# First norm of a two-block forward pass: order of the squares' adds, engine of one weight split, place of the norm's spread

## The chip, the cores and the metric

The kernel runs on one core of one Trainium2 chip. The metric is the device time of one execution in microseconds (us), as a median of several runs. The core has a matrix engine (TensorE, PE in the profile), a vector engine (VectorE, DVE), an activation engine (ScalarE, ACT), a general engine (GpSimd, POOL) and a queue that starts transfers (SyncE, SP). Each engine works through its own list of instructions in order, and semaphores hold an instruction back until what it needs is there.

## The reference

A sequence of 512 tokens of width 1024 goes through two blocks. Only the beginning of the first block is touched by the change:

```python
h = rmsnorm(x, ln1[l])
z = jnp.einsum('btd,de->bte', h, w_in[l])
u_pool, gq, gk, gv, gg, ga, fq, fk, fv, ff = jnp.split(z, pts, axis=-1)
y_pool = pool_mixer(u_pool, w_pool[l], pool_scale[l])
y_gla = gla_mixer(gq, gk, gv, gg, ga, w_a_up[l], b_a[l], gla_gn[l])
y_fox = fox_mixer(fq, fk, fv, ff, b_f[l])
mix = jnp.concatenate([y_pool, y_gla, y_fox], axis=-1)
x = x + jnp.einsum('btd,de->bte', mix, w_o[l])
```

`rmsnorm` divides each token by the root of the mean of its squares and multiplies by a gain. `gq`, `gk`, `gv` are the query, key and value of a gated linear attention, `ga` is the low-rank input of its decay gate, which is multiplied by `w_a_up`. The rest (a feed-forward layer, a second block with two more attentions) is left as it is.

## The kernel before, in words

Activations lie transposed: 8 tiles of 128 channels by 512 tokens, `x0` to `x7`. Every fp32 operand of a product is split in two: a rounded high part, made by ScalarE (L188), and the remainder, made by VectorE or GpSimd (L189), so that one product costs three matmuls (high by high, low by high, high by low). A weight slab (128 by 1024) is loaded by SyncE into one of two raw buffers `wr`, then split into `wh` and `wl`, of which there are three each (`weight`, L194 to L203). By default every second slab has its remainder made on GpSimd, the others on VectorE (`share` is 2 there). A raw buffer is free for the next transfer when both halves of its split are done.

The norm is not applied before the products. The products run on x times the gain, and their results are multiplied by the reciprocal root afterwards. For that the squares are summed: ScalarE squares each tile (L294, L297), VectorE adds seven of them into `ss` (L298), TensorE sums `ss` over its channels with eight one-column matmuls against `ones` (`col_sum`), ScalarE and VectorE make the reciprocal root `col` and split it in two `part` tiles (`inv_sqrt`, `parts`), TensorE spreads it over the 128 partitions with eight matmuls against `identr` (`spread`), and ScalarE copies the result to a tile `R` (L280). `R` multiplies every product by channel, `col` every product by token.

TensorE's order is written out by hand. Products on the first slabs run while the sums are made: the small slab of the gates (`psg`), the query slab (`psq`), then five of the eight steps of the key slab (`XS`); then the column sums; then the rest of the key slab, with the spread in between; then the value product by token (`gla_v`), whose slab is in two halves `w1gv`. After the first two steps of it (six matmuls) comes the matmul of the gate, `ga` by `wau`, which needs `R`: VectorE adds the two halves of the gate product into a tile `b` (L581), and multiplies it by `R` into `ga` (L582).

The other engines' lists are ordered by a scheduler, which works with modelled times, with two means to move it: `high_priority`, and `issue_after`, which queues an instruction behind a given one on its engine.

Of the kernel before, what the change touches and what calls it, by code (L numbers as in the profile page):

```python
# [11 lines left out]
F32 = mybir.dt.float32  # L12
# [4 lines left out]
OP = mybir.AluOpType  # L17
# [67 lines left out]
class Body:  # L85
# [179 lines left out]
    def parts(self, c):  # L265

        n = c.shape[1]
        hi, lo = (self.gp.tile([P, 8], F32R, tag="part", name="part", bufs=6)[:, :n] for _ in "hl")
        self.nc.vector.tensor_copy(hi, c)
        self.nc.vector.tensor_tensor(lo, c, hi.bitcast(F32), op=OP.subtract)  # L270
        return hi, lo

    def spread(self, parts):

        ps = self.bank("tr")
        for t in range(NT):
            for a, c in enumerate(parts):
                self.mm(ps[:, t * P:(t + 1) * P], c[:, t:t + 1].to_broadcast([P, P]), self.identr, a == 0, a == 1)
        r = self.row()
        self.nc.scalar.activation(r, ps, AF.Copy)  # L280
        return r

    def rstd(self, sums, n):
        with self.tc.high_priority():
            c = self.inv_sqrt(self.col_sum(sums)[0], n)
            parts = self.parts(c)
        yield RSW
        with self.tc.high_priority():
            return self.spread(parts), c

    def square_into(self, ssum, src, first, scale=1.0, eng=None):
        nc = self.nc
        if first:
            nc.scalar.activation(ssum, src, AF.Square, scale=scale)  # L294
        else:
            sq = self.tmp()
            nc.scalar.activation(sq, src, AF.Square, scale=scale)  # L297
            (eng or nc.gpsimd).tensor_tensor(ssum, ssum, sq, op=OP.add)  # L298

    def acts(self):  # L300
        return [tuple(self.hp.tile([P, T], F32R, name=f"{c}{k}", tag=f"{c}{k}") for c in ("hh", "hl"))
# [172 lines left out]
    def block1(self, ctx, raw):  # L474
        nc, A, x = self.nc, self.A, self.x
        mp = self.pool(ctx, "mix")
        mix = [tuple(mp.tile([P, T], F32R, name=f"m{c}{k}") for c in "hl") for k in range(4)]
        b = lambda dt=F32: mp.tile([P, T], dt, tag="b", name="b", bufs=NB)

        wg = self.wp.tile([P, 1024], F32R, tag="wh", name="wh", bufs=3)  # L480
        wg3, raw3 = wg.rearrange("p (k m) -> p k m", m=P), raw[:, :512].rearrange("p (k m) -> p k m", m=64)
        self.split(wg3[:, :, :64], wg3[:, :, 64:], raw3)
        rq = self.wp.tile([P, 1024], F32, tag="wr", name="wr", bufs=WR)
        wq = [self.wp.tile([P, 1024], F32R, tag=t, name=t, bufs=3) for t in ("wh", "wl")]
        h = self.acts()
        ssum = self.sums()
        for k in range(KD):
            for n, at in enumerate((XA, XB)):
                if k == at:
                    cols = slice(n * 512, n * 512 + 512)  # L490
                    nc.sync.dma_start(rq[:, cols], A["w1s"][T1["gq"]][:, cols])
                    self.split(*(w[:, cols] for w in (*wq, rq)))
            nc.sync.dma_start(x[k], A["xT"][k * P:(k + 1) * P, :])
            last = nc.scalar.activation(h[k][0], x[k], AF.Identity, scale=self.gain("ln1", k))
            nc.vector.scalar_tensor_tensor(h[k][1], x[k], self.gain("ln1", k), h[k][0].bitcast(F32),  # L495
                                           op0=OP.mult, op1=OP.subtract)
        self.ident = self.const(self.gp, "ident", [P, P])
        self.identr = self.gp.tile([P, P], F32R, name="identr")
        nc.scalar.activation(self.identr, self.ident, AF.Copy)
        for k in range(KD):  # L500
            with self.tc.issue_after(getattr(last, "ins", last)):
                self.square_into(ssum, x[k], k == 0, eng=nc.vector)
        self.identb = self.const(mp, "identb", [P, P], BF16)
        self.causalb = self.const(mp, "causalb", [P, P], BF16)
        psg = self.bank("mm")
        gen = self.dense(wq, h)
        for k in range(KD):
            for half in (True, False) if k == KD - 1 else (False, True):
                if half:
                    self.mm(psg[:64], wg3[:, k, :64], h[k][1], False, False)  # L510
                else:
                    self.mm(psg, wg3[:, k, :], h[k][0], k == 0, k == KD - 1)
            if k >= XL:
                next(gen)
        psq = self.all(gen)
        gen = self.dense(self.slab("w1s", T1["gk"]), h)
        for _ in range(XS):
            next(gen)
        r = self.rstd([ssum], D)
        next(r)  # L520
        next(gen)
        next(gen)
        R, Rc = self.all(r)
        psk = self.all(gen)
        fd = self.dp.tile([8, T], F32, name="fd")
        V = [[], []]
        proj = self.fox_proj(h, R, b)
        with ExitStack() as c:
            self.gla_phase(c, h, R, Rc, mix, mp, b, fd, psg, (psq, psk), V, proj)
        self.share = 1  # L530
        with ExitStack() as c:
            xp = self.pool(c, "mix2")
            mix += [tuple(xp.tile([P, T], F32R, name=f"m{c}{k}") for c in "hl") for k in range(4, KD)]
            self.fox_phase(mp, b, mix, V, fd, proj, self.half_zero(xp))
            self.share = 2
            h2 = self.acts()
            ssum = self.sums()
            for m in range(KD):
                self.all(self.w_o(mix, m, 1))
                self.split_scaled(h2[m][0], h2[m][1], x[m], self.gain("ln2", m))  # L540
                self.square_into(ssum, x[m], m == 0, eng=nc.vector if m == KD - 1 else nc.gpsimd)
            self.last = [ssum]
        self.h = h2
# [8 lines left out]
    def gla_phase(self, ctx, h, R, Rc, mix, mp, b, fd, psg, held, V, proj):  # L552
        nc, A = self.nc, self.A
# [23 lines left out]
        def gates():  # L577

            z, t = new()[:64], self.tmp()[:64]
            nc.scalar.activation(t, psg[64:], AF.Copy)  # L580
            nc.vector.tensor_tensor(z, psg[:64], t, op=OP.add)  # L581
            nc.vector.tensor_tensor(ga, z[:16], R[:16], op=OP.mult)  # L582
            f = new()[:8]
            nc.vector.tensor_tensor(f, z[32:40], R[32:40], op=OP.mult)
            F = self.log_sigmoid(f, self.gain("b_f", 0, 8), 8, new)
            one = new()[:8]
            nc.gpsimd.memset(one, 1.0)
            nc.vector.tensor_tensor_scan(F, one, F, 0.0, op0=OP.mult, op1=OP.add)
            nc.sync.dma_start(fd, F)

        def gla_v():
            yield from self.take()
            w = [self.weight(A["w1gv"][a]) for a in range(2)]
            for t in range(NT):
                ps = yield from self.token_major(h, t, w)
                nc.vector.tensor_scalar(gv[t], ps[:, :256], Rc[:, t:t + 1], None, op0=OP.mult)
                if t < NT - 1:
                    yield
            self.busy = False
# [117 lines left out]
        def chain(f, held=None):  # L717
            if f == 0:
                gates()
            q, k = yield from qk(f, held)  # L720
            yield QKW
            r = decay(f, q, k)
            yield DECW
            sb = yield from state(f, r)
            gs[f] = yield from gate(f)
            yield GOW
            yield from output(f, r, sb, gs[f])
# [28 lines left out]

        self.spawn(chain(0, held))
        self.later("gv", gla_v(), 2 * UNIT)
        self.spawn(chain(1), CH1)
        self.spawn(pooling(0), PL0)  # L760
# [718 lines left out]
```

## Time and profile before

| | us |
|---|---|
| three runs | 1077.87, 1076.41, 1077.69 |
| median | 1077.69 |
| the profiled execution, its own time | 1081.27 |
| its span, first to last instruction | 1079.5 |
| TensorE busy in it | 1048.9 (97%) |
| VectorE busy in it | 671.8 (62%) |
| ScalarE busy in it | 545.5 (51%) |
| GpSimd busy in it | 366.8 (34%) |

Mean granted TensorE clock is 0.990 of full speed. A row of the timeline gives the start from the span's beginning, the duration, the engine, the line, the operation with the tiles written and read, and in brackets the idle time before it with what ended it. Rows of several instructions (x3) are merged: their duration runs from the first start to the last end. Matmuls overlap each other, so the distance between starts tells their pace, not their duration.

### The profile page before, as it was taken

To read this page: it belongs to the slowest core of one execution; us is meant where nothing else is said; L and a number is where in the kernel's file an instruction comes from. 1 tells how busy PE (TensorE), PEld (TensorE's weight loads), DVE (VectorE), ACT (ScalarE), POOL (GpSimd) and SP (SyncE) were. 2 spreads that over 40 slices of the span, in tenths; PEclk is the share of its full clock that TensorE was granted. 3 is DMA by queue.
4 is the path that set the end of the run, shared out by engine and by line. 5 is a ranking of instruction groups with operands and counts; after the bars stand their busy time and mean duration, and the time that the engine had idled before them with its cause. 6 is when DMAs were issued, how large, how long until landed. Compare 5 with 4: busy or idle time off the path is not lost.

```text
span 1079.5 us, 14066 instructions
## 1 busy us (share of the span) xinstructions
PE 1048.9 (97%) x5264; PEld 868.8 (80%) x5264; DVE 671.8 (62%) x1140; ACT 545.5 (51%) x954; POOL 366.8 (34%) x214
## 2 busy tenths in 40 slices
PE   8999999999999999999999998989899999999997
PEld 6888877788888888888888787768787898888786
DVE  6653488885545423454533278999995566888652
ACT  6763578755323211333244465656565556778233
POOL 1233322143222100232223243443334336655354
PEclk9999999999999999999999999989999999999999
DMA  6312132152222232323223143232232323335842
GB/s 229 99 59 79 63 102 64 66 185 98 98 98 97 83 104 84 110 89 102 88 95 108 40 144 131 90 108 88 74 100 86 117 78 118 109 99 163 287 144 79
DMA packets 41692, 114.84 MB, mean 106 GB/s; under 512 B 4952, under 2 KB 9448, under 8 KB 41624
## 3 DMA queue, kind: packets, MB, share of 16 engines
q1 hardware_dynamic: 38536, 107.62, 30.6%
q10 hardware_dynamic: 2448, 4.22, 1.0%
q0 software_dynamic: 640, 2.10, 0.5%
q8 instruction: 42, 0.69, 0.3%
q14 instruction: 26, 0.21, 0.1%
HBM read 103.40 MB, written 13.14 MB: 108 GB/s over the span
## 4 chain that ended last, share of the span: by engine, by line
PE 79%; DVE 14%; ACT 2%; issue 2%; DMA 1%; SPq 0%; DVEq 0%; ACTq 0%
PE mm L151 67%; PE sc L151 4%; PE pv L151 3%; PE tr L151 2%; PE tr L158 2%; DVE kst L189 2%; DVE score L1016 1%; DVE m L1015 1%; DVE pl L387 1%; DVE b L311 1%; DVE b L374 1%; DVE qk L189 1%; DVE s L369 1%; DVE s L1069 1%; DVE b L369 1%
## 5 line engine op out<-in xcount | busy, mean ns | idle before, releaser
L189 POOL TENSOR_TENSOR wl<-wr,wh 128x1024 fp32r<-128x1024 f32 (+2 forms) x107 | 262.5, 2454 | 565.7 <-ACT wh L188 525.6
L151 PE MATMUL mm<-hh,wh 128*128 128x512 f32 (+2 forms) x808 | 325.5, 403 | 1.6 <-DVE z L1087 1.6
L151 PE MATMUL mm<-hl,wh 128*128 128x512 f32 (+3 forms) x808 | 316.9, 392 | 0.5 <-DVE hl L495 0.5
L151 PE MATMUL mm<-hh,wl 128*128 128x512 f32 (+1 forms) x800 | 314.3, 393 | 0.0
L188 ACT ACTIVATE wh<-wr 128x1024 fp32r<-128x1024 f32 (+2 forms) x142 | 146.8, 1034 | 217.1 <-PE mm L151 181.8
L151 PEld LDWEIGHTS mm<-hh,wh 128*128 128x128 f32 (+1 forms) x808 | 153.4, 190 | 33.4 <-DVE z L1087 2.0
L151 PEld LDWEIGHTS mm<-hh,wl 128*128 128x128 f32 (+1 forms) x800 | 151.2, 189 | 32.8
L151 PEld LDWEIGHTS mm<-hl,wh 128*128 128x128 f32 (+2 forms) x808 | 152.9, 189 | 28.7 <-DVE hl L495 1.2
L151 PE MATMUL mm<-fh,wdh 128*128 128x512 f32 x176 | 70.1, 398 | 0.0
L151 PE MATMUL mm<-fl,wdh 128*128 128x512 f32 x176 | 69.6, 395 | 0.0
L151 PE MATMUL mm<-fh,wdl 128*128 128x512 f32 x176 | 69.6, 395 | 0.0
L188 ACT ACTIVATE wdh<-wd 128x1408 fp32r<-128x1408 f32 x16 | 22.1, 1381 | 72.1 <-PE mm L151 68.1
L875 DVE TENSOR_TENSOR u<-mm,R 128x512 f32<-128x512 f32 x22 | 15.2, 691 | 68.3 <-PE mm L151 68.3
L880 DVE TENSOR_TENSOR x<-mm,x 128x512 f32<-128x512 f32 x16 | 11.1, 692 | 73.3 <-PE mm L151 73.3
L387 DVE TENSOR_TENSOR pl<-tr,ph 128x128 fp32r<-128x128 f32 (+1 forms) x96 | 46.0, 483 | 11.3 <-ACT ph L386 10.2
L189 DVE TENSOR_TENSOR fl<-u,fh 128x512 fp32r<-128x512 f32 x22 | 42.1, 1914 | 14.7 <-ACT fh L188 14.7
L371 ACT ACTIVATE s<-s,m 128x128 f32<-128x128 f32 (+1 forms) x64 | 35.7, 558 | 25.5 <-DVE m L369 25.2
L298 POOL TENSOR_TENSOR ss<-ss,t 128x512 f32<-128x512 f32 x21 | 30.8, 1479 | 52.0 <-ACT t L297 51.9
L189 DVE TENSOR_TENSOR wl<-wr,wh 128x1024 fp32r<-128x1024 f32 (+1 forms) x34 | 40.8, 1199 | 9.4 <-ACT wh L188 9.3
L151 PE MATMUL mm<-wh,hh 128*128 128x256 f32 x160 | 46.5, 290 | 0.0
L151 PE MATMUL mm<-wl,hh 128*128 128x256 f32 x160 | 45.2, 283 | 0.0
L386 ACT ACTIVATE ph<-tr 128x128 fp32r<-128x128 f32 (+1 forms) x96 | 40.5, 427 | 9.4 <-PE tr L158 8.7
(341 smaller groups left out, 2019.1 us busy)
## 6 DMA issues: line engine op xcount, KB each, us to landing
wr<-in_w1gu SPq DMA_DIRECT2D x44, 512.0 KB, 3.5
wr<-in_w2s SPq DMA_DIRECT2D x39, 512.0 KB, 3.5
wd<-in_w1d SPq DMA_DIRECT2D x16, 704.0 KB, 4.2
wr<-in_w1s SPq DMA_DIRECT2D x15, 512.0 KB, 3.5
wr<-in_w1o SPq DMA_DIRECT2D x8, 512.0 KB, 3.5
wr<-in_w2o SPq DMA_DIRECT2D x8, 512.0 KB, 3.8
shear<-gd SPq DMA_DIRECT2D x1, 2560.0 KB
x<-in_xT SPq DMA_DIRECT2D x8, 256.0 KB, 4.9
```

The costliest lines, as they stand in the source:

```text
L151: self.nc.tensor.matmul(out, l, r, start=start, stop=stop)
L158: self.nc.tensor.transpose(out, src, self.ident if ident is None else ident)
L188: self.nc.scalar.activation(hi, src, AF.Copy)
L189: (eng or self.nc.vector).tensor_tensor(lo, src, hi.bitcast(F32), op=OP.subtract)
L298: (eng or nc.gpsimd).tensor_tensor(ssum, ssum, sq, op=OP.add)
L311: nc.vector.tensor_tensor(q[x:x + 64], qf[o:o + 64], q[o:o + 64].bitcast(F32), op=OP.subtract)
L369: nc.vector.tensor_tensor_reduce(out=s[:, :n], in0=sc[:, :n], in1=bias(i), op0=OP.add, op1=OP.min, scale=1.0, scalar=3e38, accum_out=m[:, ...
L371: nc.scalar.activation(s[:, :n], s[:, :n], AF.Exp, scale=-1.0, bias=m[:, 0:1], accum_out=m[:, 1:2])
L386: nc.scalar.activation(hi, trv, AF.Copy)
L387: nc.vector.tensor_tensor(lo, trv, hi.bitcast(F32), op=OP.subtract)
L875: nc.vector.tensor_tensor(u, ps, self.R2, op=OP.mult)
L880: nc.vector.tensor_tensor(x[m], ps, x[m], op=OP.add)
```

## The change

Three edits, all in the first 30 us. The adds of the squares get high priority. The two halves of the value slab are both split on VectorE (`pool=False`), the first behind the last add of a square, the second behind the split of the reciprocal root; the gate's add `b` is put behind that split too. And the spread of the root is issued after the third part of the products (the whole key slab) instead of before its last step.

```diff
     def parts(self, c):
...
-        self.nc.vector.tensor_tensor(lo, c, hi.bitcast(F32), op=OP.subtract)
+        last = self.nc.vector.tensor_tensor(lo, c, hi.bitcast(F32), op=OP.subtract)
+        self.parted = getattr(last, "ins", last)
         return hi, lo
...
     def square_into(self, ssum, src, first, scale=1.0, eng=None):
...
-            (eng or nc.gpsimd).tensor_tensor(ssum, ssum, sq, op=OP.add)
+            return (eng or nc.gpsimd).tensor_tensor(ssum, ssum, sq, op=OP.add)
...
         for k in range(KD):
-            with self.tc.issue_after(getattr(last, "ins", last)):
-                self.square_into(ssum, x[k], k == 0, eng=nc.vector)
+            with self.tc.high_priority(), self.tc.issue_after(getattr(last, "ins", last)):
+                add = self.square_into(ssum, x[k], k == 0, eng=nc.vector)
+        self.added = getattr(add, "ins", add)
...
         r = self.rstd([ssum], D)
         next(r)
-        next(gen)
-        next(gen)
+        psk = self.all(gen)
         R, Rc = self.all(r)
-        psk = self.all(gen)
...
             nc.scalar.activation(t, psg[64:], AF.Copy)
-            nc.vector.tensor_tensor(z, psg[:64], t, op=OP.add)
+            with self.tc.issue_after(self.parted):
+                nc.vector.tensor_tensor(z, psg[:64], t, op=OP.add)
...
         def gla_v():
             yield from self.take()
-            w = [self.weight(A["w1gv"][a]) for a in range(2)]
+            w = []
+            for a, first in enumerate((self.added, self.parted)):
+                with self.tc.issue_after(first):
+                    w.append(self.weight(A["w1gv"][a], pool=False))
```

On TensorE one thing moves: the eight matmuls of the spread (`tr<-identr,part`), in the difference of the two lists.

```order
 L151 MATMUL mm<-hl_148,wh 128x512
 L151 MATMUL mm<-hh_147,wl 128x512
-L151 MATMUL tr<-identr,part 128x128 x8
 L151 MATMUL mm<-hh_149,wh 128x512
 L151 MATMUL mm<-hl_150,wh 128x512
 L151 MATMUL mm<-hh_149,wl 128x512
+L151 MATMUL tr<-identr,part 128x128 x8
 L151 MATMUL mm<-wh,hh_135 128x256
 L151 MATMUL mm<-wl,hh_135 128x256
```

The last three matmuls of the key slab stand ahead of the spread now, and the value product (`mm<-wh,hh`) directly behind it.

On VectorE, from the last add of a square on, before the change (`wl_370` is the second half of the value slab, `b_339` the gate's add, `col` and `part` the reciprocal root and its split):

```order
L298 TENSOR_TENSOR ss_151<-ss_151,t_205 128x512
L581 TENSOR_TENSOR b_339<-mm_212,t_340 64x512
L189 TENSOR_TENSOR wl_370<-wr_367,wh_369 128x1024
L262 RECIPROCAL col_281<-col_281 128x4
L269 CAST part_284<-col_281 128x4
L270 TENSOR_TENSOR part_285<-col_281,part_284 128x4
L582 TENSOR_TENSOR ga_326<-b_339,R_303 16x512
```

And with the change (`wl_364` is the first half of the value slab):

```order
L299 TENSOR_TENSOR ss_151<-ss_151,t_205 128x512
L189 TENSOR_TENSOR wl_364<-wr_361,wh_363 128x1024
L262 RECIPROCAL col_281<-col_281 128x4
L269 CAST part_284<-col_281 128x4
L270 TENSOR_TENSOR part_285<-col_281,part_284 128x4
L582 TENSOR_TENSOR b_339<-mm_212,t_340 64x512
L189 TENSOR_TENSOR wl_370<-wr_367,wh_369 128x1024
L583 TENSOR_TENSOR ga_326<-b_339,R_306 16x512
```

The first half's split has come over from GpSimd, whose list now begins, after its memsets, with the split of the next slab, `wl_512`; the gate's add and the second half's split stand behind the root. The split of the key slab (`wl_257`, not shown) stays where it was, between the third and the fourth add.

On ScalarE, before (`wh_369` is the second half of the value slab, `wh_511` the next slab, the second query slab):

```order
L188 ACTIVATE wh_369<-wr_367 128x1024
L261 ACTIVATE col_281<-tr_276,eps_86 128x4
L280 ACTIVATE R_303<-tr_294 128x512
L188 ACTIVATE wh_511<-wr_509 128x1024
L431 ACTIVATE b_346<-b_344,gains_82 8x512
```

And with the change:

```order
L188 ACTIVATE wh_369<-wr_367 128x1024
L261 ACTIVATE col_281<-tr_276,eps_86 128x4
L188 ACTIVATE wh_511<-wr_509 128x1024
L281 ACTIVATE R_306<-tr_297 128x512
L432 ACTIVATE b_346<-b_344,gains_82 8x512
```

The high part of the next slab now stands ahead of the copy of `R`. SyncE's list keeps its order; its transfer of that next slab waits for VectorE and ScalarE (the first half's split) instead of GpSimd. Behind these places the lists of all engines are the same as before.

## Rows read from the trace of the kernel before

**Rows 1.** Chain that ended last, in order of time, 17 to 21 us: start, duration, what.

```profile
17.28 0.70 DVE ss L298
...
18.07 2.85 DVE ss L298
...
21.01 0.70 DVE ss L298
```

**Rows 2.** Timeline of TensorE, 20 to 29 us: start, duration, engine, line, operation.

```profile
20.32 0.39 PE L151 MATMUL mm<-hh,wl 128*128 128x512 f32 x1
21.76 1.05 PE L151 MATMUL tr<-ones,ss 128*128 128x1 f32 x8 [1.05 <-DVE ss L298]
22.67 0.48 PE L151 MATMUL mm<-hh,wh 128*128 128x512 f32 x1
22.99 0.40 PE L151 MATMUL mm<-hl,wh 128*128 128x512 f32 x1
...
24.89 1.80 PE L151 MATMUL tr<-identr,part 128*128 128x128 f32 x8
26.49 0.55 PE L151 MATMUL mm<-hh,wh 128*128 128x512 f32 x1
...
27.35 0.28 PE L151 MATMUL mm<-wh,hh 128*128 128x256 f32 x1
...
28.15 1.12 PE L151 MATMUL tr<-ga,c_wau 16*128 16x512 f32 x2
```

**Rows 3.** Timeline of GpSimd, 17 to 32 us.

```profile
17.97 2.40 POOL L189 TENSOR_TENSOR wl<-wr,wh 128x1024 fp32r<-128x1024 f32 x1 [14.45 <-DVE ss L298]
28.45 2.56 POOL L189 TENSOR_TENSOR wl<-wr,wh 128x1024 fp32r<-128x1024 f32 x1 [8.09 <-ACT wh L188]
```

**Rows 4.** Windows by engine, with granted clock third from the end, DMA share, GB/s.

```profile
23.26:26.66 3.40, 3.40 (x14) 3.01 (x13) 0.59 (x4) 0.00 (x0) 0.00 (x0) 0.50 0.49 160
...
690.57:692.17 1.60, 0.00 (x1) 0.00 (x1) 1.60 (x3) 0.00 (x0) 0.39 (x1) 1.00 0.19 26
692.17:696.00 3.83, 3.83 (x17) 3.19 (x18) 3.83 (x6) 2.88 (x5) 2.86 (x2) 1.00 0.25 79
...
706.73:712.26 5.53, 5.53 (x14) 4.37 (x15) 5.36 (x20) 2.56 (x6) 0.59 (x1) 0.50 0.15 58
...
814.77:817.08 2.31, 0.00 (x0) 0.00 (x0) 2.06 (x4) 0.77 (x2) 1.39 (x2) 1.00 0.51 204
818.56:821.98 3.42, 3.42 (x9) 2.68 (x9) 2.50 (x3) 1.20 (x4) 1.88 (x1) 0.50 0.14 32
```

**Rows 5.** Timeline of VectorE, 22 to 30 us.

```profile
22.22 1.21 DVE L189 TENSOR_TENSOR wl<-wr,wh 128x1024 fp32r<-128x1024 f32 x1
...
23.76 0.16 DVE L270 TENSOR_TENSOR part<-col,part 128x4 fp32r<-128x4 f32 x1
27.36 0.68 DVE L582 TENSOR_TENSOR ga<-b,R 16x512 f32<-16x512 f32 x1 [3.44 <-ACT R L280]
...
29.98 1.31 DVE L434 TENSOR_SCALAR b<-b,gains 8x512 f32<-8x512 f32 x1
```

**Rows 6.** Timeline of ScalarE, 17 to 43 us.

```profile
17.79 0.62 ACT L297 ACTIVATE t<-x 128x512 f32<-128x512 f32 x1
...
26.73 0.60 ACT L280 ACTIVATE R<-tr 128x512 f32<-128x512 f32 x1 [3.62 <-PE tr L151]
27.32 1.06 ACT L188 ACTIVATE wh<-wr 128x1024 fp32r<-128x1024 f32 x1
...
41.26 1.99 ACT L188 ACTIVATE wh<-wr 128x1024 fp32r<-128x1024 f32 x2
```

**Rows 7.** Timeline of SyncE's queue, 20 to 21 us.

```profile
20.39 0.33 SPq L197 DMA_DIRECT2D wr<-in_w1s  x1
```

**Rows 8.** The page's DMA issues: count, size, median us from issue to landing.

```profile
wr<-in_w1s SPq DMA_DIRECT2D x15, 512.0 KB, 3.5
```

## The prediction, made before the changed kernel was run

> **What bounds the kernel now.** I read the chain of waits first, in order of time, and only as far as the change reaches. Between 12 and 21.7 us it runs through ScalarE's squares and VectorE's adds; from the column sums on it stays on TensorE. So here the start of a TensorE instruction sets the end, and whatever TensorE is given back or made to wait at 20 to 30 us goes through to the end, since the later gaps follow from work that hangs on TensorE itself.
>
> The chain shows one add of 2.85 us among adds of 0.70 [rows 1]. GpSimd's timeline shows why: its split of the first value half runs from 17.97 to 20.37, and the add that began at 18.07 ends 0.55 us after it [rows 1, 3]. TensorE's timeline shows the price: the column sums begin at 21.76 after 1.05 us idle [rows 2]. The table by windows shows a second price: from 23.26 to 26.66 the granted clock is 0.50, the lower of the two levels, 1.2 instead of 2.4 GHz [rows 4]. Just before it fell TensorE had idled 1.05 us and then spent 0.91 us on one-column matmuls.
>
> **The adds and the value half.** The fourth add begins at 16.48 in the chain, starts are 0.80 apart, the last square is ready at 18.41 [rows 1, 6]. Without the split on GpSimd the last add ends at 16.48 + 3 × 0.80 + 0.70 = 19.58. That is ahead of TensorE, which is free for the column sums at 20.32 + 0.23 = 20.55, the pace of the products being 0.23. The wait goes: 21.76 − 20.55 = 1.21 us earlier. The high priority changes nothing that I can see: the key slab's split still stands among the adds. The value half's split costs VectorE 1.21 us [rows 5], from 19.5 to 20.7; nothing hurries behind it, as the reciprocal root cannot come before 22.
>
> **Up to the spread.** The column sums take 0.91 (21.76 to 22.67), so the key products start at 21.46. At full clock the nine take 0.32 + 8 × 0.23 = 2.16 [rows 2]; the spread begins at 23.62. The parts of the root were ready 2.16 us after the column sums began (21.76 to 23.92) [rows 2, 5], so now at 22.71: no wait. The spread took 1.60 us at half clock (24.89 to 26.49) and so about 0.80 at full, an estimate from that row; it ends at 24.42, against 26.49 before. If it all went on like this, over 2 us would be won.
>
> **What is late next: the gate.** Behind the spread TensorE had three key products and six value matmuls to do (26.49 to 28.15, where the gate's matmul waited a tenth at most). Now only the six value matmuls are left, 0.12 each (six in the 0.80 from 27.35 to 28.15, the last with its tail), and TensorE stands at the gate's matmul at 25.14. That matmul needs `ga`, and `ga` needs `R`. Before, this took 28.15 − 26.49 = 1.66 us from the spread's end. Two things now lengthen it.
>
> First, ScalarE makes the high part of the next slab ahead of `R`. Its transfer was issued at 20.39, when GpSimd ended the first half [rows 3, 7]; now VectorE ends it at about 20.70, issue at 20.72, and with 3.5 us to landing [rows 8] ScalarE begins at 24.22 and ends at 25.28 (1.06 us [rows 6]). `R` follows, 25.28 to 25.88. It cannot be much earlier: that buffer is also still read by the key products until 23.6.
>
> Second, GpSimd's remainder of the same slab starts 0.07 us after ScalarE's part (28.38 to 28.45 [rows 3, 6]), so at 25.35, before `R` is there, and runs 2.40 us to 27.75. `ga` reads `b` and `R`, both in SBUF, as the slow add read two tiles in SBUF. In the same way an 8-partition step (L434, a tile and a column, from SBUF to SBUF), begun at 29.98 while GpSimd's split ran to 31.01, took 1.31 us and ended 0.28 after it [rows 3, 5]; so a small operand gives no cover. I let `ga` end 0.55 us after GpSimd, at 28.30, and the gate's matmul begin 0.11 later (28.04 to 28.15 before), at 28.41. That is 0.26 us later than before. From both sides: with the slab landing early the split ends at 27.15 and it is −0.34; with `ga` not blocked at all it is −1.46 (below). I take +0.26, since the blocked add is the nearest row.
>
> The Trainium skill (SBUF — State Buffer, Who interferes with whom) states it as a rule: a VectorE instruction with two SBUF inputs contends with a GpSimd instruction that reads SBUF, and whichever issues first keeps the ports for its whole length, whatever its shape. The add of 2.85 us agrees; no row here shows `ga` itself in that place. By the rule the sum is the one above, by a shared port it would be the rival without a block.
>
> **The clock once more.** TensorE now idles from 25.14 to 28.41, 3.27 us, ahead of a matmul that uses 16 partitions. After an idle 2.31 us at 814.77 the clock fell to 0.50 for 3.42 us of work; after 1.60 us at 690.57 it stayed at 1.00 [rows 4]. At half clock half the time is lost: 1.71 us by the first. Bounds: nothing by the second, 2.8 us by the longest stretch at 0.50 (706.73 to 712.26). I take 1.7, as the gap is longer than 2.31. The drop of before at 23.26 lies ahead of 28.15 and is already in that start.
>
> **Edits at nothing.** The gate's add moves behind the root, done at 23.3; the value product, which needs its PSUM bank, comes at 24.42; without that cover TensorE would wait for it. The second value half is split by 24.5, a microsecond later; its matmuls stand behind the gate's. The transfer that waits for it goes out a microsecond later, for a slab that ScalarE takes at 41.26 [rows 6].
>
> **Sum.** +0.26 + 1.71 = +2.0 us on the profiled execution: span 1079.5, own time 1081.27 (1.8 us around it), so 1083.3 there. The runs' median lies 3.6 us lower, and the same difference gives 1077.69 + 2.0 = 1079.7 us.
>
> **Rivals.**
> - *Block, but the clock stays.* Only the 0.26 is left: 1078.0. For it: 690.57 kept its clock. Against: that gap is half as long.
> - *No block (the other side).* `ga` runs beside GpSimd's split: `R` at 25.88, `ga` to 26.58, the gate's matmul at 26.69, −1.46; the idle of 1.55 us is like 690.57, so no drop: 1076.2. Without the wait for the slab either, the gate's matmul comes at 24.42 + 1.46 = 25.9: −2.3, 1075.4. It decides itself by whether GpSimd's split has begun when `R` is there. For it: both follow from the same ScalarE instruction, half a microsecond apart. Against: that half microsecond is always in GpSimd's favour.
> - *The runs timed before had no drop at 23.26.* Then the gate's matmul stood at 26.5 in them, 1.6 us earlier than in the trace, and the change costs 2.0 + 1.6 = 3.6 us: 1081.3. For it: one execution's trace proves one drop. Against: two of three runs lie within 0.2 us at the upper end.
> - *The adds do not get faster*, some other work slowing them: column sums again at 21.76, the block then ends later than before too; about +1 to +3, inside the slower cases.
>
> **How the numbers follow.** My forecast has 0.58, with 1078.8 to 1080.9 as its own range; block without drop 0.13; no block 0.16; no drop before 0.13 (the last rival in it). 0.2%, what a measurement can tell here, is 2.16 us: slower begins at 1079.85. The forecast lies close below that and gives 0.26 of its 0.58 to slower, with 0.13 from the third rival 0.39. Faster than 1075.5 takes the best end of the no-block case and something I do not see: 0.07. Within is 0.54. The range from 1075.8 to 1082.0 leaves out the last bit of the no-block case and a doubled drop.
>
> **What would show it.** Right: no idle before the column sums, which start near 20.55; full clock at 23 to 25; ScalarE's `wh` ahead of `R`; GpSimd's split starting near 25.4; `ga` of 2 us or more, or starting when GpSimd ends; TensorE idle about 3 us before the gate's matmul; a granted clock of 0.50 soon after. Wrong: `ga` of 0.68 us while GpSimd runs, or `R` before the slab's high part has begun, or a clock of 1.00 from 25 to 40 us.

## The result, and the profile after

The changed kernel is slower: 1086.09 us as a median of 4 runs (1085.34 to 1088.72), against 1077.78 as a median of 4 runs of the kernel before: the three of the table above, and one more of 1079.96. The ratio on record is 1.0057, 95% interval 1.0031 to 1.0083; that is what 1086.09 over 1079.96 gives, while the two medians would give 1.0077. The forecast was 1079.7 us with a range of 1075.8 to 1082.0, most of its chance on no measurable difference. The profiled execution took 1086.31 us (span 1084.3), the one of before 1081.27 (1079.5).

At the start nearly everything stands where the prediction put it. TensorE, 20 to 31 us, answers to [rows 2]:

```profile
20.62 0.95 PE L151 MATMUL tr<-ones,ss 128*128 128x1 f32 x8
23.61 1.00 PE L151 MATMUL tr<-identr,part 128*128 128x128 f32 x8
24.45 0.33 PE L151 MATMUL mm<-wh,hh 128*128 128x256 f32 x1
...
25.09 0.28 PE L151 MATMUL mm<-wh,hl 128*128 128x256 f32 x1
28.41 2.07 PE L151 MATMUL tr<-ga,c_wau 16*128 16x512 f32 x2 [3.04 <-DVE ga L583]
```

The column sums start 1.14 us earlier and without a wait, the spread 1.28 us earlier. Then TensorE idles 3.04 us, and the gate's matmul comes at 28.41, which is 0.26 later than in the trace of before.

VectorE shows why, ahead of that matmul and behind it [rows 1, 5]:

```profile
16.59 3.07 DVE L299 TENSOR_TENSOR ss<-ss,t 128x512 f32<-128x512 f32 x4
19.57 1.22 DVE L189 TENSOR_TENSOR wl<-wr,wh 128x1024 fp32r<-128x1024 f32 x1
...
25.91 2.44 DVE L583 TENSOR_TENSOR ga<-b,R 16x512 f32<-16x512 f32 x1 [1.71 <-ACT R L281]
28.39 0.68 DVE L585 TENSOR_TENSOR b<-b,R 8x512 f32<-8x512 f32 x1
```

The last four adds take 3.07 us together, none of them 2.85. But `ga`, 0.68 us before, takes 2.44. The next instruction, with half its partitions and alone again, takes 0.68.

ScalarE's high part of the next slab, and behind it the copy of `R` [rows 6]:

```profile
24.34 1.06 ACT L188 ACTIVATE wh<-wr 128x1024 fp32r<-128x1024 f32 x1 [2.47 <-DMA wr<-in_w1s]
25.30 0.57 ACT L281 ACTIVATE R<-tr 128x512 f32<-128x512 f32 x1
```

And GpSimd, whose first split [rows 3] is gone and whose split of that slab begins ahead of `ga`:

```profile
25.48 2.34 POOL L189 TENSOR_TENSOR wl<-wr,wh 128x1024 fp32r<-128x1024 f32 x1 [21.96 <-ACT wh L188]
```

It ends at 27.82, `ga` at 28.35, 0.53 us after it; for the slow add of before that distance was 0.55. The Trainium skill (SBUF — State Buffer, Who interferes with whom) states that the order of issue and not the shape of the operation decides who is blocked. The operand of 16 partitions agrees, at 2.44 us instead of 0.68.

The chain that ended last therefore runs through the next slab and not through the root (columns: start, duration, what):

```profile
19.66 1.15 DVE wl L189
...
20.87 3.38 DMA wr<-in_w1s
...
24.34 1.06 ACT wh L188
25.40 0.49 ACT R L281
...
25.91 2.46 DVE ga L583
...
28.41 2.07 PE tr L151 x2
```

What was not forecast in this size is the clock. The windows (busy time of each engine, and third from the end the granted clock) answer to [rows 4]:

```profile
25.37:28.41 3.04, 0.00 (x2) 0.00 (x1) 2.47 (x2) 0.51 (x2) 2.79 (x2) 0.98 0.46 160
28.41:35.14 6.73, 6.73 (x24) 5.23 (x25) 3.56 (x6) 5.29 (x7) 0.00 (x0) 0.50 0.21 78
35.14:41.36 6.22, 6.22 (x54) 6.22 (x54) 5.64 (x10) 3.67 (x7) 0.00 (x0) 1.00 0.09 26
...
1009.54:1011.15 1.61, 0.00 (x1) 0.00 (x0) 1.56 (x1) 0.00 (x0) 1.01 (x1) 1.00 0.97 299
1011.15:1014.56 3.41, 3.41 (x8) 2.67 (x9) 1.28 (x2) 0.00 (x0) 0.56 (x1) 0.53 0.88 325
```

For 6.73 us behind the idle time TensorE ran at the lower level, 1.2 GHz: twice the length of the drop of before at 23.26. 24 matmuls fit in there; the next 54 needed 6.22 us at 2.4 GHz. A second drop at 1011.15 is in this trace and in neither the first trace of before nor the repetition of the changed kernel below. It does not belong to the change: the kernel with the value half alone (below) has it too, from 1006.75 us in its trace, at the same place of the program.

### The profile page after: what moved, and what is told of

It reads as the page before. It is cut to its first block, busy times and chain, and to the rows that moved or that the text cites. A ratio compares the mean times of both kernels' runs of the same rounds, so it can differ in the third digit from the quotient of the medians.

```text
span 1084.3 us, 14067 instructions
## 1 busy us (share of the span) xinstructions
PE 1049.9 (97%) x5264; PEld 870.0 (80%) x5264; DVE 670.6 (62%) x1141; ACT 545.7 (50%) x954; POOL 365.0 (34%) x213
## 4 chain that ended last, share of the span: by engine, by line
PE 78%; DVE 15%; ACT 3%; issue 2%; DMA 2%; SPq 0%; DVEq 0%; ACTq 0%
PE mm L151 67%; PE sc L151 4%; PE pv L151 3%; PE tr L151 2%; PE tr L158 2%; DVE score L1020 2%; DVE kst L189 1%; DVE m L1019 1%; DVE pl L388 1%; DVE b L312 1%; DVE b L375 1%; DVE qk L189 1%; DVE s L370 1%; DVE s L1073 1%; DVE b L370 1%
## 5 line engine op out<-in xcount | busy, mean ns | idle before, releaser
L189 POOL TENSOR_TENSOR wl<-wr,wh 128x1024 fp32r<-128x1024 f32 (+1 forms) x106 | 261.2, 2465 | 572.5 <-ACT wh L188 548.4
L879 DVE TENSOR_TENSOR u<-mm,R 128x512 f32<-128x512 f32 x22 | 15.2, 691 | 68.2 <-PE mm L151 68.2
L151 PE MATMUL mm<-wh,hl 128*128 128x256 f32 x160 | 46.1, 288 | 0.0
```

Source lines behind the costliest of these rows:

```text
L151: self.nc.tensor.matmul(out, l, r, start=start, stop=stop)
L189: (eng or self.nc.vector).tensor_tensor(lo, src, hi.bitcast(F32), op=OP.subtract)
L879: nc.vector.tensor_tensor(u, ps, self.R2, op=OP.mult)
```

## How the runs were told apart

Ten runs of eight kernels follow, in the order of the sections below, each beside runs of the kernel before on the same chip. Two measures of the traces and runs are used throughout.

The first is the distance of a fixed instruction from its place in the second trace of before. ScalarE loads its activation table 15 times in a run, at the same places of the program in all versions. The start of five of these loads, in us, against that trace:

```
load at (second trace of before)   29.03   55.53   260.20   617.45   1053.00
before, first trace                +1.07   +1.11    +1.15    +1.24     +0.06
before, third trace                -0.89   -0.89    -0.89    -0.90     -1.81
changed, first trace               +2.19   +4.38    +4.40    +4.43     +4.89
changed, second trace              +1.81   +3.30    +3.36    +3.43     +4.29
before + spread moved              +1.91   +3.38    +3.47    +3.54     +4.37
changed + products in the gap      +1.86   +1.87    +1.87    +1.85     +2.55
changed, spread in old place       -1.58   -1.60    -1.53    -1.46     -2.26
  the same, second trace           -1.23   -1.23    -1.16    -1.09     -1.07
```

One entry needs care. In the first trace of the changed kernel the first of these loads, at 31.22 us, already stands inside the drop, so its +2.19 holds a part of the drop. The gate's matmul, with which the drop begins, is +1.38 there (28.41 against 27.03). In the second trace (28.84) and with the spread moved alone (28.93) it is +1.81 and +1.90, as the loads say.

The second uses all runs. Each run has its span and its mean granted clock; span times (1 - clock) is the time lost to the clock, and the rest of the span is everything else. The means, in us (each next to the kernel before on the same chip):

```
                                 span     lost to clock   rest     before: span, lost, rest
changed, first comparison (4)    1084.5       14.1       1070.4      not on record
changed, again (4 runs)          1084.3       14.4       1069.9      1079.2, 11.2, 1068.0
before + spread moved (4)        1085.2       15.7       1069.5      1079.2, 11.2, 1068.0
changed + products in gap (10)   1082.3       12.6       1069.8      1079.9, 11.4, 1068.4
changed + slab on VectorE (10)   1081.1       12.5       1068.6      1079.9, 11.4, 1068.4
changed + R first (10)           1078.9       10.9       1068.0      1079.9, 11.4, 1068.4
spread in old place (12)         1078.5       10.9       1067.6      1079.2, 11.2, 1068.0
  the same, second time (11)     1078.5       11.6       1066.9      1079.4, 11.3, 1068.1
value half alone (10)            1078.6       11.2       1067.4      1079.2, 11.2, 1068.0
before, again (10)               1078.8       10.6       1068.2      1079.9, 11.4, 1068.4
before, once more (11)           1079.4       11.5       1067.9      1079.4, 11.3, 1068.1
```

The clock is given to three digits, so one run's loss is known to half a microsecond. The last two rows compare the kernel before with itself: its means differ by up to 0.8 us in the loss and 0.2 in the rest, so differences of that size between two kernels say nothing.

## The experiments

**The kernel before, again** (no edit). Was the drop at 23.26 us usual?

> The kernel before, unchanged, for a second trace. The first trace of it had TensorE at half clock from 23.26 to 26.66 us and took 1081.27 us, while the other executions took 1076.4 to 1080.0. If that drop is an accident of one execution, this trace shows a granted clock of 1.00 from 20 to 40 us, the matmul of the gate at about 26.5 instead of 28.15, and a span near 1076. If it belongs to the kernel, the drop is there again and the gate's matmul stands near 28.15. Ratio to the runs of before within 0.998 to 1.002 either way.

1080.11 us, ratio 0.9987 (0.9975 to 1.0), which also says that 0.13% between two kernels is nothing. The drop is gone from this second trace of before, and yet its span, expected near 1076, is 1079.4, that of the first trace: what is won at the start is not left at the end. TensorE:

```profile
22.24 1.05 PE L151 MATMUL tr<-ones,ss 128*128 128x1 f32 x8 [1.01 <-DVE ss L298]
24.62 1.00 PE L151 MATMUL tr<-identr,part 128*128 128x128 f32 x8
27.03 1.12 PE L151 MATMUL tr<-ga,c_wau 16*128 16x512 f32 x2
```

The wait ahead of the column sums is the same, 1.01 us, but the spread takes its 0.84 us at 2.4 GHz, and the gate's matmul comes 4.79 us behind the start of the column sums instead of 6.39. Here are the two windows of this trace, the wait and what followed:

```profile
21.23:22.24 1.01, 0.00 (x1) 0.01 (x1) 0.91 (x3) 0.39 (x1) 0.00 (x0) 1.00 0.44 65
22.24:30.00 7.76, 7.76 (x49) 6.46 (x50) 5.73 (x10) 4.10 (x6) 2.69 (x2) 1.00 0.38 129
```

So the same wait brings a drop in one execution and none in the next.

**R's copy first.** The changed kernel, with the next slab's high part queued behind the copy of `R` on ScalarE.

```diff
-        self.nc.scalar.activation(r, ps, AF.Copy)
+        last = self.nc.scalar.activation(r, ps, AF.Copy)
+        self.spreaded = getattr(last, "ins", last)
...
+                with self.tc.issue_after(self.spreaded):
+                    w = self.weight(A["w1s"][T1["gq"] + f])
```

> The changed kernel with one thing moved: on ScalarE the copy of R goes ahead of the high part of the next weight slab, as it did before; the other engines' lists stay. By the theory that the gate's product ga is held by GpSimd's split of that slab: R ends at about 25.05, ga runs unblocked for 0.68 us, GpSimd starts after it, the gate's matmul begins near 25.9 instead of 28.41, TensorE idles 0.6 us and the clock stays at 1.00; some 5.5 us less than the changed kernel's trace. By the rival that only ScalarE's order cost time and the clock drop has another cause: 0.6 us of R's delay are won (R ends at 25.87 in the changed kernel) and the drop after 28 us stays.

1081.21 us, ratio 0.9989 (0.9974 to 1.0004). `ga` is back at its short form, and TensorE waits little:

```profile
26.27 0.68 DVE L584 TENSOR_TENSOR ga<-b,R 16x512 f32<-16x512 f32 x1 [1.08 <-ACT R L281]
...
27.26 2.65 POOL L189 TENSOR_TENSOR wl<-wr,wh 128x1024 fp32r<-128x1024 f32 x1 [23.74 <-ACT wh L188]
```

```profile
27.01 1.12 PE L151 MATMUL tr<-ga,c_wau 16*128 16x512 f32 x2 [0.64 <-DVE ga L584]
```

GpSimd now begins behind `ga`. The gate's matmul stands 5.40 us behind the start of the column sums instead of 7.79, after a wait of 0.64. One line of ScalarE's order takes the whole loss away.

**The next slab's remainder on VectorE.** The order on ScalarE stays as in the changed kernel; only GpSimd is taken out of the way.

```diff
-            nc.vector.tensor_tensor(ga, z[:16], R[:16], op=OP.mult)
+            g = nc.vector.tensor_tensor(ga, z[:16], R[:16], op=OP.mult)
+            self.gated = getattr(g, "ins", g)
...
+                with self.tc.issue_after(self.gated):
+                    w = self.weight(A["w1s"][T1["gq"] + f], pool=False)
```

> The changed kernel with the low part of the next weight slab (the second query slab) made on VectorE, queued behind the gate's product ga, instead of on GpSimd; ScalarE still makes its high part ahead of R. This takes away the block alone. By the block theory: ga takes 0.68 us from about 25.9, the gate's matmul begins at 26.7, TensorE idles 1.3 us instead of 3.0; with the clock at 1.00 some 4.7 us less than the changed kernel's trace, 1.7 if it still falls. By the rival (ScalarE's order is the cost, GpSimd is harmless): ga still ends near 28.35 and nothing is won.

1083.18 us, ratio 1.0010 (0.9999 to 1.0020).

```profile
24.59 1.06 ACT L188 ACTIVATE wh<-wr 128x1024 fp32r<-128x1024 f32 x1 [2.44 <-DMA wr<-in_w1s]
25.56 0.58 ACT L281 ACTIVATE R<-tr 128x512 f32<-128x512 f32 x1
```

```profile
26.16 0.68 DVE L583 TENSOR_TENSOR ga<-b,R 16x512 f32<-16x512 f32 x1 [1.68 <-ACT R L281]
```

```profile
26.90 1.12 PE L151 MATMUL tr<-ga,c_wau 16*128 16x512 f32 x2 [1.24 <-DVE ga L583]
```

`R` still stands behind the slab, but `ga` takes 0.68 us. The gate's matmul comes 6.00 us behind the start of the column sums: 1.8 earlier than in the changed kernel, 0.60 later than with `R` first. That splits the delay: 1.8 us is the block by GpSimd, 0.6 is ScalarE's order. The clock stays at 1.00 from 20 to 40 us in this trace and in that with `R` first.

**Products in the gap.** The changed kernel, with eight extra products into an unused bank ahead of the gate's matmul, so that the wait stays and TensorE idles less.

```diff
+            if k == 1 and fill:
+                junk = self.bank("pv")
+                for _ in range(fill):
+                    self.nc.tensor.matmul(junk, act[0][0][:, :P], act[0][0], start=True, stop=True)
```

> The changed kernel with 8 products more on TensorE, into an unused PSUM bank, between the sixth value matmul and the gate's matmul: 1.8 us of work in the 3.0 us in which TensorE idled. Nothing else moves. ga is blocked as before, so the gate's matmul begins at 28.41 in every theory. If the loss behind it is the clock, falling because TensorE idled, the clock stays at 1.00 and the value product ends some 3.0 us earlier; ratio to the changed kernel about 0.997. If 1.2 us of idle and the 16-partition matmul are enough, it falls all the same and the time is that of the changed kernel.

1084.59 us, ratio 1.0028 (1.0014 to 1.0042).

```profile
25.53 2.00 PE L244 MATMUL pv<-hh 128*128 128x512 f32 x8
28.89 1.12 PE L151 MATMUL tr<-ga,c_wau 16*128 16x512 f32 x2 [1.35 <-DVE ga L587]
```

```profile
27.53:28.89 1.36, 0.01 (x1) 0.00 (x1) 1.33 (x2) 0.00 (x0) 1.22 (x2) 1.00 0.04 15
28.89:36.00 7.11, 7.11 (x52) 6.35 (x53) 4.16 (x8) 6.34 (x9) 0.00 (x0) 1.00 0.23 74
```

The gate's matmul is as late as in the changed kernel (7.95 us behind the start of the column sums), the clock stays at 1.00, and the offset of +1.86 at 29 us is still +1.87 at 55 us, where the changed kernel has gone from +1.38 at the gate's matmul to +4.38. The block and the clock are two costs, and in this trace the second alone is gone. Its runs still lose 1.2 us more to the clock than before beside them, where the changed kernel loses about 3; this trace shows no drop at 20 to 40 us, so that remainder lies elsewhere or in other executions, and is not settled.

**The changed kernel, again** (no edit).

> The changed kernel, unchanged, for a second trace and more timed runs beside the others. If the idle of 3 us ahead of the gate's matmul brings the clock down every time, the trace shows it again: gate's matmul 7.8 us after the column sums began, half clock behind it for 3.4 to 6.8 us; ratio to before near 1.005. If the long drop (28.3 to 35.1 us) was an accident of one execution, the ratio comes out near 1.002.

1086.3 us, ratio 1.0051 (1.0036 to 1.0065).

```profile
25.80:28.84 3.04, 0.00 (x1) 0.00 (x1) 2.47 (x2) 0.51 (x2) 2.79 (x2) 1.00 0.45 156
28.84:30.30 1.46, 1.46 (x5) 0.70 (x6) 1.43 (x3) 0.77 (x2) 0.00 (x0) 1.00 0.63 166
30.30:33.70 3.40, 3.40 (x18) 3.40 (x18) 1.56 (x3) 3.35 (x5) 0.00 (x0) 0.51 0.20 83
```

The block repeats: TensorE idles 3.08 us by its timeline, 3.04 in the first trace, and the gate's matmul stands 7.84 us behind the start of the column sums, 7.79 in the first. The drop is half as long as in the first trace and begins 1.46 us after TensorE is back at work. It costs 1.5 us here (+1.81 to +3.30), 3.0 in the first (+1.38 at the gate's matmul to +4.38).

**Spread back in its old place**, the other two edits kept.

```diff
-        psk = self.all(gen)
+        next(gen)
+        next(gen)
         R, Rc = self.all(r)
+        psk = self.all(gen)
```

> The changed kernel with the spread back in its old place, ahead of the last step of the key slab; adds, value slab and gate's add as in the change. ScalarE's copy of R then stands ahead of the next slab again. By the block theory nothing holds ga: the gate's matmul begins 4.6 us after the column sums (7.8 in the changed kernel, 4.8 in the second trace of before), with no idle of TensorE and a clock of 1.00; the column sums start without a wait, so 1.3 us less than before, ratio near 0.999. By the rival that the value slab on VectorE does the harm (gate's add and second half behind the root) the gate's matmul stays late.

1080.67 us, ratio 0.9997 (0.9988 to 1.0006).

```profile
20.75 0.95 PE L151 MATMUL tr<-ones,ss 128*128 128x1 f32 x8
23.04 1.00 PE L151 MATMUL tr<-identr,part 128*128 128x128 f32 x8
...
25.45 1.12 PE L151 MATMUL tr<-ga,c_wau 16*128 16x512 f32 x2
```

No wait is left: the gate's matmul stands 4.70 us behind the start of the column sums. The loss is gone with this edit; the gain that was expected (0.999) is not told from none.

**The spread alone**, in the kernel before (the other side of the same edit).

> The kernel before with the spread moved behind the third product and nothing else: adds, value slab and GpSimd as before, but ScalarE's list now has the next slab ahead of R. If the move of the spread alone brings the block, ga takes 2 us or more, the gate's matmul begins 7.3 us after the column sums, which wait for the adds as before; TensorE idles 2.7 us and the clock falls; ratio 1.005 or more. If the block needs the value slab on VectorE, ga takes 0.68 us and the ratio is near 1.

1087.33 us, ratio 1.0057 (1.0043 to 1.0070): all of the loss.

```profile
21.81 1.05 PE L151 MATMUL tr<-ones,ss 128*128 128x1 f32 x8 [1.32 <-DVE ss L298]
24.87 1.00 PE L151 MATMUL tr<-identr,part 128*128 128x128 f32 x8
...
28.93 1.12 PE L151 MATMUL tr<-ga,c_wau 16*128 16x512 f32 x2 [2.29 <-DVE ga L580]
```

```profile
26.55 2.33 DVE L580 TENSOR_TENSOR ga<-b,R 16x512 f32<-16x512 f32 x1 [2.57 <-ACT R L280]
```

The slow add is still in it, and `ga` is blocked all the same, 2.33 us, for the same reason: GpSimd's split of the next slab begins at 25.98, `ga` at 26.55. The gate's matmul stands 7.12 us behind the start of the column sums, and the clock is at 0.50 from 31.31 to 34.71, which costs 1.5 us (+1.91 to +3.38).

**The value half alone.** The kernel before with both halves of the value slab split on VectorE.

```diff
-            w = [self.weight(A["w1gv"][a]) for a in range(2)]
+            w = [self.weight(A["w1gv"][a], pool=False) for a in range(2)]
```

> The kernel before with the first value half's low part on VectorE (pool=False) and nothing else: no priority, no order behind adds or root, spread in its old place. The scheduler then puts that split between the adds. If GpSimd's split was what stretched the add of 2.85 us, all adds take 0.70 us, the column sums wait at most 0.3 us instead of 1.05, the gate's matmul follows 4.8 us after them; ratio 0.999. If another cause stretched it, one add still takes over 2 us.

1080.42 us, ratio 0.9994 (0.9985 to 1.0003). Adds and column sums:

```profile
19.10 0.68 DVE L298 TENSOR_TENSOR ss<-ss,t 128x512 f32<-128x512 f32 x1
...
20.31 0.67 DVE L298 TENSOR_TENSOR ss<-ss,t 128x512 f32<-128x512 f32 x1
```

```profile
21.04 1.05 PE L151 MATMUL tr<-ones,ss 128*128 128x1 f32 x8 [0.24 <-DVE ss L298]
```

No add is slow, and the wait shrinks from 1.01 to 1.07 in the traces of before to 0.24. The rest comes from the queue: a value split and the gate's add stand between the last adds (1.22 from 17.97, 0.68 from 19.71), while in the changed kernel the first value split is queued behind the last add, and the gate's add behind the root.

**Spread back, and before, once more.** Does the earlier start show in the time?

> The changed kernel with the spread in its old place, once more, now beside a second copy of the kernel before on the same chip. Its trace had the gate's matmul at 25.45 us, 1.58 earlier than the undisturbed trace of before (27.03), and kept 1.5 us of that up to 617 us, yet its time was 0.9997 of before. Theory: those 1.6 us are real but no more than what the same kernel scatters by, so 1077.5 to 1080 us here, about 1.5 us below the copy of before, and the span less the time lost to a low clock (span times one less granted clock) 1.0 to 1.6 us lower than that of before. Rival: the gain of the start is given back later in most executions (another gap or clock drop), and span less lost clock time is within 0.5 us of before. In its trace the column sums begin at 20.6 to 21.0 and the gate's matmul 4.6 to 4.8 us after them.

> The kernel before, unchanged, once more. Both theories: ratio 1.000 within 0.0015 to the kernel before. What it is for: a third trace of before. If the column sums begin at 21.7 to 22.3 us and the gate's matmul at 26.4 to 27.1 with the clock at 1.00 until then, the drop at 23.26 us of its first trace is the exception; the theory expects that. The rival (the drop is usual) expects a granted clock of 0.50 at 23 to 27 us and the gate's matmul near 28.15.

Spread back: 1080.3 us, ratio 0.9994 (0.9985 to 1.0004). Before: 1081.2, ratio 1.0 (0.9991 to 1.0009). The third trace of before:

```profile
21.33 1.05 PE L151 MATMUL tr<-ones,ss 128*128 128x1 f32 x8 [1.07 <-DVE ss L298]
...
26.14 1.12 PE L151 MATMUL tr<-ga,c_wau 16*128 16x512 f32 x2
```

No drop, and the gate's matmul even a bit earlier than expected. Of three traces of before, one has the drop at 23 us. The start of the same kernel lies anywhere over 2 us (gate's matmul at 28.15, 27.03, 26.14), and the spans without clock loss of the two runs with the spread back lie 0.4 and 1.2 us below before. The rival expected the first of these, the theory the second. The time itself came 0.7 us below before, half of what the theory expected. A gain of up to 1 us is possible, but it is not told from no change, and no version here is shown to beat the kernel before.

## Why the prediction was wrong

Right were the steps up to the gate, and they were right in place and size.
- The adds: column sums at 20.62, 20.55 forecast, no wait. That the value half on GpSimd was what stretched the add is shown by its removal alone: no add is slow then. That the high priority changes nothing is not settled: with the value half moved alone, without the priority and the new queueing, two other instructions stand among the last adds and keep 0.24 us of the wait. Which of the two keeps them out was not tried apart.
- The spread at 23.61 (23.62 forecast), at full clock.
- The block: the high part at 24.34 (24.22), `R` at 25.30 (25.28), GpSimd at 25.48 (25.35), the gate's matmul at 28.41 (28.41). That the last one fits to the hundredth is luck: GpSimd began 0.13 later than forecast, its split was 0.06 shorter, and the second trace has 28.84. That it is GpSimd is shown by the next slab on VectorE (1.8 us earlier), that ScalarE's order lets GpSimd go first by `R` first (2.4 us earlier). The rival without a block is out: GpSimd began 0.4 to 0.6 us ahead of `ga` in all four traces that have the spread moved and this split on GpSimd behind ScalarE's order.

Two steps failed, both ones of size and not of mechanism.

The first is "The drop of before at 23.26 lies ahead of 28.15 and is already in that start", and with it the sum's +0.26. It is true of that one execution. In the other two traces of before there is no drop, and the gate's matmul comes at 27.03 and 26.14, 4.79 and 4.81 us behind the start of the column sums instead of 6.39: the drop had cost 1.6 us. Against before without the drop, the block costs 1.9 us by the runs (the rest of the span, 1069.9 against 1068.0); by the traces the gate's matmul is 1.4 to 1.9 us later than in the second trace of before, and 2.3 to 2.8 later than in the third. The third rival said so, and priced it at 1.6 us more, as measured; it was given 0.13. The 3.6 us by which the profiled execution lay above the median was no sign of that drop: the second trace of before lacks the drop and took 1081.21 us, against 1081.27.

The second is the clock's "I take 1.7", with its bound of 2.8. The idle time came as forecast (3.04 us for 3.27), and the drop behind it too. By the traces (two of the changed kernel, one of the spread alone) it cost 3.0, 1.5 and 1.5 us. The first of these can be read in the terms of the sum too: the transposes behind the value product came at 46.95 instead of 43.67 in the first trace of before, 3.28 later, of which 0.26 is the gate. By the runs of the repetition the changed kernel loses 3.2 us more to the clock than before (14.4 against 11.2). Of the eight runs of both comparisons five lost 13.0, about 1.8 more than before and near the forecast, and three 15.2 to 17.4. Both traced executions are among the five, so what brought the others so far is not shown.

The bound of 2.8 was read too short. Its row [rows 4] begins at 706.73, where TensorE took up work; the clock had fallen before that:

```profile
705.92:712.75 6.83, 6.02 (x16) 4.86 (x17) 6.63 (x23) 2.99 (x6) 1.08 (x1) 0.50 0.24 93
```

So a drop as long as the one that followed (6.73) stood in the trace of before. Half of the 6.02 us in which TensorE was busy is the 3.0 that was measured.

The two terms, 1.9 and 3.2, make up the 5.1 us between the spans (1084.3 and 1079.2) by the way they are defined, so their sum is no check of either; the sum of the forecast had 2.0. The rest of the miss is the level: the kernel before, 1077.7 us in the runs that were shown, came out at 1080.1 to 1081.9 in all later ones. The two medians of the first comparison lie 8.3 us apart; its ratio says 0.57%, and so, nearly, does the repetition beside 23 runs of before (5.4 us, 0.51%). What makes the level was not tried.

## What to carry to other kernels

Before moving an instruction to a later place, ask what its consumer's engine and that engine's partner will have started by then: here the copy of `R` slipped behind one weight slab on ScalarE, and a GpSimd split that began 0.4 us too early held the one VectorE operation that TensorE was waiting for. A stall of TensorE is priced twice, once for itself and once for the lower clock behind it, and the second can be the larger (1.9 and 3.2 us here, by the means of the runs). Before building a sum on one profiled execution, take a second one of the same kernel, and look for what only the first has: here a clock drop worth 1.6 us, which two further traces lacked.

## What the hardware showed that was not expected

- The same idle time does not always bring the same clock. 3.04 us idle was followed by 6.73 us at half clock in one execution, and 3.08 us by 3.40 in the next, which began 1.46 us after work had resumed. About 1 us idle ahead of the column sums was followed by a drop in one of three traces of before, and 1.61 us at 1009.54 by one in the first trace of the changed kernel, but 1.65 us at the same place by none in the second.
- With eight products that compute nothing the clock stayed at 1.00 in the one trace that was taken, though TensorE still idled 1.36 us behind them. That saves the 1.5 to 3.0 us of the drop there; the means of the runs have 12.6 us lost to the clock, against 14.4 in the changed kernel and 11.4 in the kernel before.
- A VectorE product of two SBUF tiles with only 16 partitions is held by GpSimd's split like a full one: 2.33 to 2.48 us in four traces, 0.68 in all others.
